# A product with zeros ahead of each group of value products, in the attention of a two-layer encoder

## The chip, the core and the metric

The kernel runs on one core of a Trainium2 chip. The metric is the device time of one execution in microseconds (us), lower being better. The other seven cores are idle.

## What is computed

The reference is a trunk of two layers over 1024 positions of width 1024. Each layer has a mixing part (a gated convolution, six heads of sparse attention, called DSA below, and six heads of banded chunk attention), a cross-attention into 256 memory tokens, and an MLP. The change touches the last product of the two attentions in the mixing part, `p` times `v`:

```python
# chunk attention, one chunk of 64 queries against a band of 9 chunks
s = jnp.einsum('bqhd,bkhd->bhqk', qc, kc).astype(jnp.float32) * scale + bias
s = jnp.where(valid, s, -jnp.inf)
p = jax.nn.softmax(s, axis=-1)
return jnp.einsum('bhqk,bkhd->bqhd', p.astype(vc.dtype), vc)
...
# DSA, one block of 128 queries against the keys that an indexer selected
p = jax.nn.softmax(s, axis=-1)
return jnp.einsum('bhqk,bqkd->bhqd', p.astype(v_sel.dtype), v_sel)
```

## The kernel before

All products run in a form of float32 that the TensorE rounds on reading (F32R), so each factor is split into a high and a low part: `split` lets ScalarE (ACT) write the high part (line 664) and VectorE (DVE) or GpSimd (POOL) subtract it from the source (line 665). An ordinary product of two split factors is three matmuls, `mm3`, lines 340 to 342. Every matmul has its own load of the stationary operand, which the profile shows as the engine PEld.

Per layer the work is: input projections together with the indexer and its top-k selection; then the attention; then the output projection, the cross-attention and the MLP. The attention stage is written as three generators merged by hand: `attention()`, the rest of the mask steps, and `memory`, which projects the memory tokens for the cross-attention and is emitted at a lower priority (`shift(FILL, ...)`) to fill TensorE's gaps.

`attention()` runs `pipeline` over units, first 24 of the chunk attention (six heads, four groups `g` of 256 queries), then 16 of DSA (eight query blocks `b`, two head groups `hg`). A unit has a `scores` part (products, a DVE step that adds the mask and finds the minimum on line 1008, exponentials on ACT on line 1014, division by the row sum on POOL on line 1025) and, three units later, a `values` part.

In `values` the work goes by groups. For one group TensorE transposes blocks of the softmax into a PSUM bank `ps` (line 1145 in the chunk units, 1260 in DSA), `split` makes `ph` and `pl` of it on ACT and DVE, and then the value products (lines 1159 and 1269) add `values x ph` and `values x pl` to the unit's bank `po`. `po` comes from a class of two banks, `ps` from a class of three. In the chunk units the groups number 1, 2, 3 and 3 for `g` = 0 to 3, nine per head, so 54 per layer. In DSA a group is one block of keys `kt`, from 0 to `b`. At the end of a unit ACT copies the lower half of `po` (line 1170 or 1277) and DVE adds the halves (line 1171 or 1284).

Which instruction stands where in an engine's queue is decided at build time: the tile framework plans the whole program with a simulated timeline (`schedule_with_timeline_sim=True`) and priorities that count up with each emitted instruction. An added instruction can therefore also move others. SBUF is handed out by the kernel's own `Arena` of `ARENA` columns; `top=True` takes the highest free place.

Of the kernel before, what the change touches and what calls it, by code (L numbers as in the profile page):

```python
# [13 lines left out]
F32 = mybir.dt.float32  # L14
# [7 lines left out]
P = 128  # L22
# [40 lines left out]
GROUPS = [(7, 6), (5, 4, 3, 2)]  # L63
RES = 10240
BASE = 16512
ARENA = 52736
GRAN = 16


# [241 lines left out]
class Kern:  # L311
    def __init__(self, ctx, tc, a):
# [4 lines left out]
        drp = ctx.enter_context(tc.tile_pool(name="dr", bufs=1, space=bass.MemoryType.DRAM))  # L317
        self.sb = Arena(self.nc, BASE, ARENA)
        self.ps = Banks(psp.tile([P, 8 * 512], F32, name="banks"))
# [25 lines left out]
    def setup(self):  # L345
        nc, sb = self.nc, self.sb
        a = self.a
        self.idf = sb.alloc(P)
        make_identity(nc, self.idf.ap)
        self.flip = sb.alloc(P)  # L350
        nc.gpsimd.memset(self.flip.ap, 0.0)
        nc.gpsimd.affine_select(
            self.flip.ap, self.flip.ap, pattern=[[1, P]], compare_op=ALU.not_equal, fill=1.0,
            base=-(P - 1), channel_multiplier=1,
        )
        self.idr = sb.alloc(P)
        nc.vector.tensor_copy(self.idr.r, self.idf.ap)

# [735 lines left out]
    def chunk_units(self, l, st):  # L1094


        nc, sb = self.nc, self.sb

        def scores(h, g, pts):
            q1, q2, kk, _, bias = st["chk", h]  # L1100
            sm = self.small(2)
            for j, bi in enumerate((2 * g, 2 * g + 1)):
                k0 = max(0, bi - 4) * P
                w = (bi + 1) * P - k0

                def products(ps, s):
                    for i, q in enumerate((q1, q2)):
                        nc.tensor.matmul(
                            ps, q.r[:, bi * P : (bi + 1) * P],
                            kk.r[:, k0 + s.start : k0 + s.stop],  # L1110
                            start=i == 0, stop=i == 1,
                        )

                pts.append(
                    self.softmax(w, products, bias.ap[:, 640 - w : 640], sm[:, j : j + 1])
                )
                if j == 0:
                    self.normalise()
                yield 0.5
            self.rows = (pts, sm)  # L1120

        def values(h, g, pts):
            vv = st["chk", h][3]
            if h % 2 == 0 and g == 0:
                st["y"][5 + h // 2] = sb.alloc(S, top=True)
            y = st["y"][5 + h // 2]
            b = (2 * g, 2 * g + 1)
            k0 = [max(0, x - 4) for x in b]

            both = list(range(k0[1], b[0] + 1))  # L1130
            one = [(kt, 0) for kt in range(k0[0], k0[1])] + [(b[1], 1)]
            groups = [[(both[0], 2)] + one] + [
                [(kt, 2) for kt in both[i : i + 2]] for i in range(1, len(both), 2)
            ]
            po = self.ps.alloc(cls="O")

            for i, group in enumerate(groups):
                ps = self.ps.alloc(cls="T")
                n, todo = 0, []
                for kt, which in group:  # L1140
                    js = (0, 1) if which == 2 else (which,)
                    c = 0 if which == 2 else which * P
                    todo.append((kt, slice(c, c + len(js) * P), slice(n, n + len(js) * P)))
                    for j in js:
                        nc.tensor.transpose(
                            ps.ap[:, n : n + P],
                            pts[j].ap[:, (kt - k0[j]) * P : (kt - k0[j] + 1) * P],
                            self.flip.ap,
                        )
                        n += P  # L1150
                ph, pl = sb.alloc(n), sb.alloc(n)
                self.split(ph.r, pl.r, ps.ap[:, :n])
                self.ps.free(ps)
                todo = [(x, kt, o, s) for kt, o, s in todo for x in (ph, pl)]
                if i == 0:

                    todo.append(todo.pop(1))
                for m, (x, kt, o, s) in enumerate(todo):
                    nc.tensor.matmul(
                        po.ap[:, o], vv.r[:, kt * P : (kt + 1) * P], x.r[:, s],  # L1160
                        start=i == 0 and m == 0,
                        stop=i == len(groups) - 1 and m == len(todo) - 1,
                    )
                sb.free(ph)
                sb.free(pl)
                yield 1.0 / len(groups)
            for x in pts:
                sb.free(x)
            low = sb.alloc(256)
            nc.scalar.copy(low.ap[0:HD, :], po.ap[HD:P, 0:256])  # L1170
            nc.vector.tensor_tensor(
                y.ap[h % 2 * HD : h % 2 * HD + HD, g * 256 : (g + 1) * 256],
                po.ap[0:HD, 0:256], low.ap[0:HD, :], op=ALU.add,
            )
            self.ps.free(po)
            sb.free(low)
            if g == 3:
                for x in st.pop(("chk", h)):
                    sb.free(x)

        for h in range(NH):
            for g in range(4):
                pts = []
                yield (
                    scores(h, g, pts), values(h, g, pts),
                    self.chunk_prepare(l, st, h + 1) if g == 1 and h + 1 < NH else None,
                    0.4 + 0.6 * min(5.0, 2 * g + 1.5),
                )

    def dsa_units(self, l, st):  # L1190


        nc, sb = self.nc, self.sb
# [61 lines left out]
        def values(b, hg, heads):  # L1255
            po = self.ps.alloc(cls="O")
            for kt in range(b + 1):
                ps = self.ps.alloc(cls="T")
                for i in range(3):
                    nc.tensor.transpose(  # L1260
                        ps.ap[:, i * P : (i + 1) * P],
                        heads[i].ap[:, kt * P : (kt + 1) * P], self.idf.ap,
                    )
                ph, pl = sb.alloc(384), sb.alloc(384)
                self.split(ph.r, pl.r, ps.ap[:, :384])
                self.ps.free(ps)
                o = slice(kt * P, (kt + 1) * P)
                for x in (ph, pl):
                    nc.tensor.matmul(
                        po.ap[:, 0:384], st["dv"].r[:, o], x.r,  # L1270
                        start=kt == 0 and x is ph, stop=kt == b and x is pl,
                    )
                sb.free(ph)
                sb.free(pl)
                yield 1.0 / (b + 1)
            low = sb.alloc(384)
            nc.scalar.copy(low.ap[0:HD, :], po.ap[HD:P, 0:384])
            if b == 0 and hg == 0:
                parts = sb.carve(S, S, S)
                y = st["ys"] = sb.tensor(parts[0].off, 3 * S, F32)  # L1280
                for f, x in enumerate(parts):
                    st["y"][2 + f] = Part(x, y[:, f * S : (f + 1) * S])
            y = st["ys"]
            nc.vector.tensor_tensor(
                y.rearrange("p (f s) -> p f s", f=3)[
                    hg * HD : (hg + 1) * HD, :, b * P : (b + 1) * P
                ],
                po.ap[0:HD, 0:384].rearrange("p (f s) -> p f s", f=3),
                low.ap[0:HD, :].rearrange("p (f s) -> p f s", f=3), op=ALU.add,
            )  # L1290
            self.ps.free(po)
            for x in heads + [low]:
                sb.free(x)
# [3 lines left out]
        for b in range(NT):  # L1297
            for hg in range(2):
                heads = []
                yield (  # L1300
                    scores(b, hg, heads), values(b, hg, heads),
                    prepare(b + 1) if hg == 0 and b + 1 < NT else None,
                    0.5 + 1.2 * (b + 1),
                )
# [866 lines left out]
```

## Time and profile before

| | us |
|---|---|
| median of three runs | 3015.66 |
| lowest and highest | 3009.02, 3018.33 |
| the profiled execution, its own time | 3017.18 |
| the profiled execution, its span | 3015.3 |
| mean granted TensorE clock in it, as a share of full speed | 0.982 |
| TensorE matmuls (PE), busy | 2890.9, 96% of the span |
| DVE, ACT, POOL busy | 2160.8, 1559.0, 1310.1 |

The span runs from the first to the last instruction; 1.9 us of the execution's time lie around it. Matmuls are pipelined, so the busy time of a line is more than what its matmuls add to the run: the distance of two starts in a row without gaps is what one costs. The two attention stages lie at 302 to 572 us and at 1792 to 2068 us; in each, the chunk units come first and DSA second.

### The profile page before, as it was taken

The numbers are of one execution on the slowest core, as the hardware profiler recorded it, in microseconds if no ns is written. First come the engines' busy times: TensorE is split into PE (matmuls) and PEld (weight loads), VectorE is DVE, ScalarE is ACT, GpSimd is POOL, SyncE is SP. The second block draws the span as 40 slices with busy tenths as digits, with TensorE's granted clock in tenths as the row PEclk, the third lists the DMA queues.
The fourth block names the chain that finished last, engine by engine and source line by source line (L and its number), as shares of the span: only waits on it lengthen the run. The fifth ranks groups of instructions, "written<-read, shape, count | busy, mean of one in ns | idle before, by whom it ended". The sixth has DMA issues, their size and how long they took to land. (4 is left out here: it accounts for less than half of the span.)

```text
span 3015.3 us, 43469 instructions
## 1 busy us (share of the span) xinstructions
PE 2890.9 (96%) x14440; PEld 2444.5 (81%) x14440; DVE 2160.8 (72%) x4333; ACT 1559.0 (52%) x3146; POOL 1310.1 (43%) x1246
## 2 busy tenths in 40 slices
PE   8999889999999999999999998999999999999998
PEld 7787788788878788888788877887888777888886
DVE  5897886582487766778957987866625877667788
ACT  5676777623234456544457767774232444554442
POOL 4614575522335553232357146754222455533223
PEclk9999999999999999999999999999999999999999
DMA  4213433331334446755412144332213354466544
GB/s 127 63 37 83 103 108 107 101 123 36 113 115 161 170 154 218 247 182 161 162 64 66 36 101 115 96 116 79 107 42 119 102 178 165 152 237 237 181 158 147
DMA packets 265440, 381.99 MB, mean 127 GB/s; under 512 B 23168, under 2 KB 141952, under 8 KB 265216
## 3 DMA queue, kind: packets, MB, share of 16 engines
q1 hardware_dynamic: 265216, 379.22, 38.8%
q8 instruction: 114, 1.87, 0.3%
q14 instruction: 110, 0.90, 0.1%
HBM read 269.56 MB, written 95.42 MB: 121 GB/s over the span
## 5 line engine op out<-in xcount | busy, mean ns | idle before, releaser
L340 PE MATMUL banks<-sb,sb 128*128 128x512 f32 (+3 forms) x3776 | 1425.2, 379 | 23.8 <-ACT sb L664 7.6
L341 PE MATMUL banks<-sb,sb 128*128 128x512 f32 (+3 forms) x3776 | 1420.4, 377 | 11.7 <-POOL sb L286 8.6
L342 PE MATMUL banks<-sb,sb 128*128 128x512 f32 (+3 forms) x3776 | 1416.1, 376 | 7.4 <-POOL sb L665 7.1
L665 POOL TENSOR_TENSOR sb<-sb,sb 128x512 fp32r<-128x512 f32 (+1 forms) x428 | 600.5, 1415 | 913.7 <-ACT sb L664 802.4
L340 PEld LDWEIGHTS banks<-sb,sb 128*128 128x128 f32 x3776 | 715.5, 190 | 156.3 <-ACT sb L664 9.9
L341 PEld LDWEIGHTS banks<-sb,sb 128*128 128x128 f32 x3776 | 715.9, 190 | 135.1 <-POOL sb L286 10.3
L342 PEld LDWEIGHTS banks<-sb,sb 128*128 128x128 f32 x3776 | 713.9, 189 | 133.2 <-POOL sb L665 9.1
L664 ACT CAST sb<-sb 128x512 fp32r<-128x512 f32 (+1 forms) x788 | 455.7, 607 | 594.3 <-PE banks L341 161.5
L286 POOL TENSOR_TENSOR sb<-sb,sb 128x512 fp32r<-128x512 f32 (+2 forms) x288 | 382.6, 1343 | 486.6 <-ACT sb L285 425.3
L665 DVE TENSOR_TENSOR sb<-sb,sb 128x512 fp32r<-128x512 f32 x360 | 274.0, 788 | 38.2 <-ACT sb L664 36.0
L665 DVE TENSOR_TENSOR sb<-banks,sb 128x384 fp32r<-128x384 f32 (+2 forms) x324 | 188.0, 595 | 88.6 <-ACT sb L664 77.0
L285 ACT CAST sb<-sb 128x512 fp32r<-128x512 f32 (+2 forms) x288 | 171.0, 607 | 134.8 <-PE banks L342 30.4
L664 ACT CAST sb<-banks 128x384 fp32r<-128x384 f32 (+2 forms) x324 | 160.1, 518 | 142.9 <-PE banks L1577 75.2
L812 DVE TENSOR_SCALAR_CACHE_REDUCE sb<-sb,sb 128x768 bf16<-128x768 f32 (+3 forms) x256 | 207.5, 810 | 5.0 <-POOL sb L443 2.0
L1741 DVE TENSOR_TENSOR sb<-sb,sb 128x512 f32<-128x512 f32 x160 | 155.2, 1005 | 61.3 <-ACT sb L1721 56.8
L1025 POOL TENSOR_SCALAR sb<-sb,sb 128x128 f32<-128x128 f32 (+7 forms) x192 | 148.5, 789 | 86.4 <-DVE sb L1023 70.0
L1783 DVE TENSOR_TENSOR sb<-banks,sb 128x512 f32<-128x512 f32 x224 | 149.5, 683 | 46.8 <-PE banks L342 45.1
L808 ACT ACTIVATE sb<-sb,sb 128x1024 bf16<-128x1024 f32 (+1 forms) x128 | 140.6, 1099 | 74.3 <-DVE sb L831 64.9
L1846 DVE TENSOR_TENSOR sb<-sb,sb 128x512 f32<-128x512 f32 x128 | 109.5, 858 | 68.7 <-DMA sb<-w_ff_dram 68.2
L1014 ACT ACTIVATE sb<-sb,sb 128x128 f32<-128x128 f32 (+7 forms) x192 | 141.9, 741 | 27.9 <-DVE sb L1008 26.8
L1720 ACT ACTIVATE sb<-sb 128x512 f32<-128x512 f32 x128 | 80.9, 632 | 115.3 <-DVE sb L1783 114.9
L1353 DVE SCALAR_TENSOR_TENSOR sb<-sb,banks 128x512 f32<-128x512 f32 x64 | 43.2, 686 | 114.0 <-PE banks L342 111.4
(173 smaller groups left out, 3055.8 us busy)
## 6 DMA issues: line engine op xcount, KB each, us to landing
sb<-h SPq DMA_DIRECT2D x236, 256.0 KB, 3.2
h<-sb SPq DMA_DIRECT2D x224, 256.0 KB, 2.2
sb<-w_ff_dram SPq DMA_DIRECT2D x216, 256.0 KB, 3.1
sb<-w_ff_dram SPq DMA_DIRECT2D x64, 512.0 KB, 4.0
sb<-w_in_dram SPq DMA_DIRECT2D x64, 256.0 KB, 2.9
sb<-w_mkv_dram SPq DMA_DIRECT2D x64, 256.0 KB, 2.7
sb<-sb SPq DMA_DIRECT2D x54, 256.0 KB, 3.7
xs<-sb SPq DMA_DIRECT2D x24, 512.0 KB, 2.8
```

The costliest lines, as they stand in the source:

```text
L285: k.nc.scalar.copy(hi, st)
L286: k.nc.gpsimd.tensor_tensor(lo, st, hi.bitcast(F32), op=ALU.subtract)
L340: mm(out, lh, rh, start=start, stop=False)
L341: mm(out, lh, rl, start=False, stop=False)
L342: mm(out, ll, rh, start=False, stop=stop)
L664: nc.scalar.copy(hi, src)
L665: eng.tensor_tensor(lo, src, hi.bitcast(F32), op=ALU.subtract)
L812: nc.vector.tensor_scalar(junkb[:, :w], x, c, None, op0=ALU.is_ge, op1=ALU.add, accum_out=n)
L1014: nc.scalar.activation(pt.ap, pt.ap, AF.Exp, bias=mn, scale=-1.0, accum_out=sm)
L1025: nc.gpsimd.tensor_scalar(pt.ap, pt.ap, rc[:, i : i + 1], 0.0, op0=ALU.mult, op1=ALU.add)
L1741: nc.vector.tensor_tensor(z.ap, x, y, op=ALU.add if spec[1] == "+" else ALU.subtract)
L1783: nc.vector.tensor_tensor(r.ap, ps.ap, part[c, x].ap, op=ALU.add)
```

## The change

A tile of zeros, 128 x 256, is made once, at the top of an arena that is larger by just those 256 columns, so the places of all other buffers can stay. In each group of a chunk unit's `values` one matmul with the same stationary block as the group's first product and the zeros as moving operand is emitted between `split` and the products. It writes columns 0 to 255 of `po`; in a unit's first group it carries the start flag, which the first product had before. In DSA the same is emitted for every block of keys but the first, without a start flag. What the other products add is unchanged, since zeros are added.

```diff
-ARENA = 52736
+ARENA = 52992
...
+        self.zero = sb.alloc(256, top=True)
+        nc.gpsimd.memset(self.zero.r.bitcast(F32), 0.0)
         self.idr = sb.alloc(P)
...
                 self.split(ph.r, pl.r, ps.ap[:, :n])
                 self.ps.free(ps)
+
+                nc.tensor.matmul(
+                    po.ap[:, 0:256], vv.r[:, todo[0][0] * P : (todo[0][0] + 1) * P],
+                    self.zero.r, start=i == 0, stop=False,
+                )
                 todo = [(x, kt, o, s) for kt, o, s in todo for x in (ph, pl)]
...
                         po.ap[:, o], vv.r[:, kt * P : (kt + 1) * P], x.r[:, s],
-                        start=i == 0 and m == 0,
-                        stop=i == len(groups) - 1 and m == len(todo) - 1,
+                        start=False, stop=i == len(groups) - 1 and m == len(todo) - 1,
                     )
...
                 o = slice(kt * P, (kt + 1) * P)
+                if kt:
+                    nc.tensor.matmul(
+                        po.ap[:, 0:256], st["dv"].r[:, o], self.zero.r, start=False, stop=False
+                    )
                 for x in (ph, pl):
```

## Rows read from the trace of the kernel before

**Rows 1.** The page: the span, then busy time, share and instructions of each engine.

```profile
span 3015.3 us, 43469 instructions
PE 2890.9 (96%) x14440; PEld 2444.5 (81%) x14440; DVE 2160.8 (72%) x4333; ACT 1559.0 (52%) x3146; POOL 1310.1 (43%) x1246
```

**Rows 2.** Busy time by stage: chunk units, DSA, first and second layer.

```profile
core 0: us, PE busy (x) PEld busy (x) DVE busy (x) ACT busy (x) POOL busy (x), PEclk, DMA share, GB/s
302.00:446.00 144.00, 124.47 (x848) 112.56 (x848) 116.84 (x331) 104.93 (x256) 89.31 (x103) 0.93 0.38 105
446.00:572.00 126.00, 121.45 (x788) 106.54 (x787) 89.58 (x235) 103.78 (x229) 65.70 (x72) 1.00 0.30 97
1792.00:1937.00 145.00, 127.40 (x851) 114.54 (x852) 119.01 (x335) 103.87 (x255) 95.76 (x107) 0.93 0.39 108
1937.00:2068.00 131.00, 122.49 (x777) 107.45 (x776) 93.85 (x239) 103.05 (x225) 69.93 (x73) 0.97 0.30 96
```

**Rows 3.** Groups by line and shape: the value products' counts, busy time and idle before.

```profile
L1269 PE MATMUL banks<-sb,sb 128*128 128x384 f32 x288 | 94.7, 381 | 8.4 <-DVE sb L665 3.9 <-ACT sb L664 3.2
L1159 PE MATMUL banks<-sb,sb 128*128 128x256 f32 x288 | 70.1, 328 | 7.7 <-ACT sb L664 4.3 <-DVE sb L665 3.1
L1159 PE MATMUL banks<-sb,sb 128*128 128x128 f32 x144 | 29.7, 274 | 9.8 <-DVE sb L665 9.5
```

**Rows 4.** Timeline in DSA: first and last of 26 matmuls of 256 columns in a row.

```profile
498.08 0.28 PE L341 MATMUL banks<-sb,sb 128*128 128x256 f32 x1
...
501.08 0.28 PE L342 MATMUL banks<-sb,sb 128*128 128x256 f32 x1
```

**Rows 5.** Busy time, as Rows 2, in stretches within the chunk units.

```profile
302.00:352.00 50.00, 40.63 (x258) 35.72 (x258) 45.34 (x135) 39.23 (x95) 27.15 (x36) 0.90 0.33 89
352.00:372.00 20.00, 19.83 (x165) 19.45 (x164) 12.36 (x33) 10.17 (x20) 9.32 (x12) 1.00 0.61 136
400.00:420.00 20.00, 19.08 (x164) 18.84 (x163) 13.33 (x37) 13.11 (x30) 17.91 (x17) 1.00 0.49 148
1792.00:1848.00 56.00, 45.77 (x282) 39.54 (x283) 51.41 (x149) 40.46 (x99) 30.70 (x37) 0.91 0.34 92
1848.00:1864.00 16.00, 16.00 (x134) 15.89 (x133) 9.28 (x25) 8.46 (x17) 9.77 (x10) 1.00 0.66 146
1888.00:1912.00 24.00, 23.35 (x181) 21.84 (x179) 19.63 (x50) 14.96 (x37) 16.56 (x15) 1.00 0.30 94
```

**Rows 6.** The same stretches, line 1159 alone: PE, PEld, clock, DMA share, GB/s.

```profile
352.00:372.00 20.00, 5.16 (x31) 4.05 (x29) 1.00 0.61 136
400.00:420.00 20.00, 4.20 (x25) 3.34 (x25) 1.00 0.49 148
1848.00:1864.00 16.00, 4.43 (x24) 3.48 (x24) 1.00 0.66 146
1888.00:1912.00 24.00, 4.47 (x28) 3.94 (x28) 1.00 0.30 94
```

**Rows 7.** What ended idle time before line 1269: us, times (matmul and load each).

```profile
  DVE sb L665: 15.3, 37
  ACT sb L664: 10.0, 17
```

**Rows 8.** Busy time, as Rows 2, in 4 us stretches around falls of the clock.

```profile
316.00:320.00 4.00, 2.43 (x17) 2.43 (x18) 4.00 (x11) 3.46 (x9) 3.02 (x4) 0.89 0.13 37
320.00:324.00 4.00, 3.20 (x17) 3.05 (x15) 4.00 (x12) 3.01 (x7) 0.98 (x1) 0.69 0.09 15
...
432.00:436.00 4.00, 0.91 (x4) 0.50 (x4) 4.00 (x8) 1.68 (x7) 1.08 (x3) 0.89 0.00 0
436.00:440.00 4.00, 3.54 (x20) 3.54 (x20) 3.05 (x13) 2.01 (x6) 1.23 (x3) 0.50 0.03 12
```

**Rows 9.** Timeline of DVE and PE around the longest stall before value products.

```profile
433.54 2.29 DVE L886 TENSOR_TENSOR_SCAN sb<-sb 128x1024 f32<-128x1024 f32 x1
435.74 0.67 DVE L665 TENSOR_TENSOR sb<-banks,sb 128x512 fp32r<-128x512 f32 x1
...
436.46 2.29 PE L1159 MATMUL banks<-sb,sb 128*128 128x128 f32 x9 [3.48 <-DVE sb L665]
```

**Rows 10.** POOL's timeline at the start of the run.

```profile
1.94 0.29 POOL L352 TENSOR_SCALAR_AFFINE_SELECT sb<-sb 128x128 f32<-128x128 f32 x1
5.23 3.13 POOL L286 TENSOR_TENSOR sb<-sb,sb 128x296 fp32r<-128x296 f32 x4 [3.01 <-ACT sb L285]
```

**Rows 11.** Waits of PE in 1792 to 2072 us: total, times, longest.

```profile
PE banks L1159 <- DVE sb L665: 6.3, 7, 2.1
PE banks L1108 <- DVE sb L1008: 5.8, 7, 2.4
```

## The prediction, made before the change was run

> **What bounds the kernel now.** I read the page first. TensorE's matmuls are busy for 2890.9 of 3015.3 us [rows 1]: over the run as a whole an added matmul can find little idle time. But the change lies only in the two attention stages, so the next view is busy time by stage. There the reader is to see how the four parts differ: in the chunk units PE is busy for 124.47 of 144 us and 127.40 of 145 us, in DSA for 121.45 of 126 and 122.49 of 131 [rows 2]. Idle PE time is thus 19.5 + 4.6 + 17.6 + 8.5 = 50.2 us, 37.1 of it in the chunk units and 13.1 in DSA. The third view is the chunk units in finer stretches. They fall in two kinds. From 302 to 352 us and from 1792 to 1848 us VectorE is the fuller engine (45.34 of 50 and 51.41 of 56 us) and PE the emptier (40.63 and 45.77). In four other stretches PE leaves 0.17, 0.92, 0 and 0.65 us free of 20, 20, 16 and 24 [rows 5]; that is where the low-priority memory projection fills it. The fourth view is the line of the value products: PE stands idle 7.7 + 9.8 us before line 1159 and 8.4 us before line 1269 [rows 3], waiting for the split on ACT and DVE, as the list of waits says too [rows 11]. The longest of these stalls, 3.48 us, came after a DVE scan of 2.29 us that stood ahead of the split in DVE's queue [rows 9]. Last, the granted clock: 0.93, 1.00, 0.93 and 0.97 in the four parts [rows 2], so it falls from 2.4 to 1.2 GHz now and then, each time after a stretch in which PE had stood idle [rows 8].
>
> **The change part by part.** *How many.* Chunk: 9 groups for each of 6 heads and 2 layers, 108 zero products. The 288 + 144 products of line 1159 [rows 3] are four per group, which agrees. DSA: 288 products of line 1269 [rows 3] are two per block of keys, so 144 blocks; those with kt = 0 (8 query blocks x 2 head groups x 2 layers = 32) get none, which leaves 112. Together 220 matmuls of 256 columns, each with a load.
>
> *What one costs.* The nearest row is a chain of 26 matmuls of 256 columns, each with its own load, without gaps: first start 498.08, last 501.08, so 3.00 us / 25 = 0.120 us [rows 4]. At full price 220 x 0.120 = 26.4 us. From below the bound is nothing, where PE would have waited anyway.
>
> For this price the Trainium skill (TensorE: Matmul & The Clock Gate, Back-to-back issue gap) gives columns / 2.4 plus 2.5 ns for a single matmul, 109 ns at 256 columns. By that the full price would be 24.0 us. The row above was taken with the loads in between, as here, and is the one I use.
>
> *Chunk units.* A zero product needs the values, the zeros and the bank, not the split. It can run as soon as the group's transposes have, in the time in which PE waits for the split; the wait then ends when it did before. In the four full stretches there is no such time: 31 + 25 + 24 + 28 = 108 products [rows 6], 27 groups, x 0.120 = 3.2 us, at full price (they have 1.7 us of room [rows 5]). The other 108 - 27 = 81 groups would cost 9.7 us in full and nothing if hidden; PE has 37.1 - 1.7 = 35.4 us of room there [rows 2, 5], and DVE is the fuller engine. But PE also releases DVE: a zero product ahead of some other transposes or scores delays what DVE and ACT get next. I take a third, 3.2 us, nearer to nothing because DVE has least room in the two largest stretches, and keep 0 and 9.7 for the range.
>
> *DSA.* 112 x 0.120 = 13.4 us in full. PE is 95% busy here (243.9 of 257 us [rows 2]). What can hide a zero product is a stall before its own value products: 37 + 17 = 54 entries are listed for line 1269, for loads and matmuls apart [rows 7], so about 27 stalls for 112 groups, a quarter. The rest, 85 x 0.120 = 10.1 us, is on the path. The ends are 0 (all of it in the 13.1 us of room) and 13.4.
>
> *The clock.* Zero products are work in stretches that have little of it. What the falls cost can be bounded by the parts' mean clock: 0.07 x 144 + 0.07 x 145 + 0.03 x 131 = 24.2 us of full-speed PE time [rows 2]. Some of it is free already, since DVE was busy all the time while the clock was low (4.00 of 4 us from 320 to 324 [rows 8]). Many falls follow one long stall, as at 432 us, where PE was busy for 0.91 of 4 us [rows 8]; a zero product of 0.12 us does not make that stretch full. I count 3 us gained, a few falls fewer; the ends are 0 and 24.2.
>
> *The rest.* The zeros are one POOL step at the start. The nearest row, a POOL step of 128 x 128, takes 0.29 us and is followed by 3.01 us of idle time [rows 10]: nothing, and at most some 0.6 us if the cover were gone. Buffers keep their places. No DMA is added or moved. The first zero product of a unit takes over the wait for the bank `po` that its first product had; behind it on PE stand the next transposes and scores, but there are two such banks, so it should be free. Finally the build-time plan: 220 more matmuls shift its clock, and a long DVE step such as the scan may come to stand before a split or no longer do so. One such stall is worth up to 3.48 us [rows 9]. I expect no sign and give it 6 us either way.
>
> *Sum.* 3.2 + 3.2 + 10.1 - 3 = 13.5 us. The profiled execution took 3017.18 us (span 3015.3), so it becomes 3030.7; it lay 1.5 us above the median of the runs, 3015.66, which becomes 3029.2. I predict **3029 us**.
>
> **The rivals.** *All hidden.* If the splits on ACT and DVE set the pace through the whole stage, the 50.2 us of PE room [rows 2] take in 26.4 us of zero products, and the falls avoided pay for the rest: 3015 to 3018 us. For it speak the stalls before the value products; against it DSA, where ACT and DVE are less busy than PE (103.78 and 89.58 against 121.45 us [rows 2]).
>
> *The clock pays.* This is the case on the other side, faster than before. If the zero products keep the clock up through most stalls, up to 24.2 us of PE time come back. At a gain of 24.2 us, with the price above, the time is 3015.7 + 16.5 - 24.2 = 3008 us; with the chunk price hidden as well, 3015.7 + 10.1 - 24.2 = 3002 us. It decides from the point where the falls avoided give back more than the 16.5 us paid, two thirds of all the clock lost in the stage. For it: in some stretches the clock fell after a moderate gap only (PE busy for 2.43 of 4 us at 316 to 320 [rows 8]), and two groups of zero products there would add 0.24 us. Against it: falls like that at 432 us, with no value product in the idle stretch, and low-clock time that DVE covers.
> The Trainium skill (TensorE: Matmul & The Clock Gate, What's actually happening) says that the throttled state is the default and that activity releases it. By that rule this rival is the one to happen, as far as the zeros count as activity; the falls after idle stretches agree with it, and no row of before shows a product with zeros.
>
> *Full price and more.* If the plan puts the zero products where PE was not waiting, all 220 cost 0.120 us, 26.4 us, and no fall is avoided: 3015.7 + 26.4 = 3042 us; if the moved plan also adds two long stalls of 3.48 us [rows 9], 3049. Against it speaks the room that PE has in the chunk units.
>
> *It does not do what it says.* If the plan were to put the zero products far from the stalls, for instance all of a unit's at its start, the stalls would stay as they are and the price be the one of the rival before.
>
> **How the numbers follow.** Partly hidden, as summed: 0.43. All hidden: 0.23. The clock pays: 0.17. Full price, wherever the zero products stand: 0.17. A measurement of this kernel can tell about 0.3% from no change, 9.0 us, so "same" is 3006.6 to 3024.7. The forecast's own spread is about 8 us (6 for the plan, a few for the shares chosen), which puts somewhat over a quarter of it, 0.12, below 3024.7. Faster: more than half of the clock's 0.17 and a little of the hidden case, 0.13. Same: 0.21 + 0.12 + 0.06 = 0.39. Slower: 0.31 + 0.17 = 0.48. The likeliest case alone spans 3019 to 3039. To leave out no more than 2 in 10, the range goes down to 3005, well into the clock's gain, and up to 3044, over the full price.
>
> **What would show it.** Two new groups in the profile, 108 and 112 matmuls of 256 columns, and 14660 matmuls instead of 14440. Line by line: the idle time before lines 1159 and 1269 should shrink by a few us, the zero products standing before it; DSA (126 and 131 us) should lengthen by about 5 us in each layer, the chunk part (144 and 145) by about 3; the mean clock of the chunk parts should rise from 0.93 by about 0.01 only. Outside the two attention stages nothing should change. I am wrong if DSA does not lengthen (then ACT and DVE set its pace), if the clock in the chunk units goes near 1.00 and the stage shortens, or if a stage without zero products changes by more than a few us, which would be the plan.

## The result, and the profile after

| | us |
|---|---|
| before, median of six runs | 3016.99 |
| after, median of six runs (3028.28 to 3034.88) | 3030.53 |
| after / before | 1.0052, 95% interval 1.0038 to 1.0065 |

The change makes the kernel slower by 13.5 us at the medians, 11 to 20 us by the interval. (The ratio is taken over the runs; that of the two medians is 1.0045.) 3029 was forecast. The sum was right to 2 us; the experiments show that its terms were not.

The page of after, its span and its busy times, answers to [rows 1]:

```profile
span 3027.5 us, 43898 instructions
PE 2905.0 (96%) x14660; PEld 2464.1 (81%) x14660; DVE 2177.8 (72%) x4333; ACT 1561.4 (52%) x3146; POOL 1302.5 (43%) x1247
```

There are 220 more matmuls, as counted, but PE is busy for only 14.1 us more. The groups by line and shape of after answer to [rows 3]. Line 1157 is the zero product of the chunk units and 1275 that of DSA; the value products stand on lines 1166 and 1279 now.

```profile
L1279 PE MATMUL banks<-sb,sb 128*128 128x384 f32 x288 | 98.8, 375 | 7.8 <-ACT sb L666 3.4 <-DVE sb L667 3.3
L1166 PE MATMUL banks<-sb,sb 128*128 128x256 f32 x288 | 71.3, 310 | 5.4 <-DVE sb L667 3.1 <-ACT sb L666 2.0
L1157 PE MATMUL banks<-sb,sb 128*128 128x256 f32 x108 | 33.4, 311 | 1.6 <-DVE sb L1177 1.6
L1275 PE MATMUL banks<-sb,sb 128*128 128x256 f32 x112 | 32.3, 288 | 0.0
L1166 PE MATMUL banks<-sb,sb 128*128 128x128 f32 x144 | 27.9, 260 | 4.2 <-DVE sb L667 3.7
```

The idle time before the chunk units' value products fell from 17.5 to 9.6 us, before DSA's from 8.4 to 7.8. A new wait of 1.6 us stands before line 1157: the first zero product of a unit waiting for its bank, which line 1177 (1171 before) reads. Few zero products stand where the change meant them to: in the trace of after 7 of the 108 in the chunk units, and none of the 112 in DSA, have a wait of TensorE of over 0.05 us straight behind them. The others are followed by the next product at once.

Next the busy time by stage. Here the stages are cut at events and not at round numbers, so that kernels can be compared: from the first score product to the last addition of the chunk units, then to the last addition of DSA, in both layers. Columns as in [rows 2]. First the kernel before, then after.

```profile
297.30:443.50 146.20, 126.34 (x847) 113.74 (x848) 116.94 (x337) 104.99 (x256) 90.70 (x102) 0.91 0.39 108
443.50:579.90 136.40, 131.83 (x836) 115.06 (x835) 98.19 (x248) 106.76 (x236) 68.98 (x75) 1.00 0.30 97
1788.20:1939.20 151.00, 131.65 (x874) 117.50 (x874) 123.78 (x346) 109.52 (x269) 97.69 (x109) 0.93 0.39 107
1939.20:2068.50 129.30, 120.59 (x762) 105.92 (x762) 91.97 (x236) 101.68 (x222) 70.43 (x73) 0.97 0.31 99
sum 562.90, PE 510.41 PEld 452.22 DVE 430.89 ACT 422.94 POOL 327.80; mean PE 127.60 PEld 113.06 DVE 107.72 ACT 105.74 POOL 81.95
```

```profile
297.60:445.70 148.10, 131.61 (x914) 117.76 (x914) 122.97 (x347) 109.17 (x265) 91.46 (x104) 0.96 0.39 107
445.70:586.90 141.20, 135.02 (x883) 122.03 (x884) 96.85 (x238) 104.06 (x226) 66.47 (x74) 1.00 0.30 94
1799.20:1950.10 150.90, 132.56 (x927) 116.97 (x927) 125.84 (x348) 110.58 (x269) 94.45 (x109) 0.99 0.40 107
1950.10:2083.60 133.50, 123.32 (x820) 111.94 (x818) 92.79 (x234) 103.11 (x222) 70.95 (x73) 0.98 0.30 96
sum 573.70, PE 522.52 PEld 468.69 DVE 438.45 ACT 426.92 POOL 323.33; mean PE 130.63 PEld 117.17 DVE 109.61 ACT 106.73 POOL 80.83
```

The two attention stages grew from 562.9 to 573.7 us. DSA grew by 4.8 and 4.2 us, about the 5 expected in each layer; the chunk units by 1.9 and -0.1, less than the 3 expected. Two things don't fit. The granted clock in the chunk units rose from 0.91 and 0.93 to 0.96 and 0.99, far more than the 0.01 I wrote. And the stretch between the two attention stages, where there is no zero product, went from 1208.3 us (579.9 to 1788.2) to 1212.3 (586.9 to 1799.2).

### The profile page after: what moved, and what is told of

Same layout as the page of the kernel before. It is cut to its first block, busy times and chain, and to the rows that moved or that the text cites. A ratio compares the mean times of both kernels' runs of the same rounds, so it can differ in the third digit from the quotient of the medians.

```text
span 3027.5 us, 43898 instructions
## 1 busy us (share of the span) xinstructions
PE 2905.0 (96%) x14660; PEld 2464.1 (81%) x14660; DVE 2177.8 (72%) x4333; ACT 1561.4 (52%) x3146; POOL 1302.5 (43%) x1247
## 5 line engine op out<-in xcount | busy, mean ns | idle before, releaser
L341 PE MATMUL banks<-sb,sb 128*128 128x512 f32 (+3 forms) x3776 | 1421.3, 377 | 13.5 <-POOL sb L286 10.4
L1751 DVE TENSOR_TENSOR sb<-sb,sb 128x512 f32<-128x512 f32 x160 | 155.8, 1009 | 58.1 <-ACT sb L1731 54.0
L1856 DVE TENSOR_TENSOR sb<-sb,sb 128x512 f32<-128x512 f32 x128 | 117.5, 921 | 66.8 <-DMA sb<-w_ff_dram 66.7
L1010 DVE CUSTOM_DVE_ANT_0 sb<-banks,sb 128x128 f32<-128x128 f32 (+5 forms) x192 | 96.3, 508 | 44.7 <-PE banks L1110 17.6
```

The costliest lines, as they stand in the source:

```text
L341: mm(out, lh, rl, start=False, stop=False)
L1751: nc.vector.tensor_tensor(z.ap, x, y, op=ALU.add if spec[1] == "+" else ALU.subtract)
```

## The experiments

The theory on record was the sum: about 0.12 us for each zero product where TensorE is full, nothing where it waits, and a plan that moves with no sign. The rivals were that the moved plan makes the time, and that the clock pays. The kernel before that a run is compared with was timed on the same chip.

**The priorities alone.** The tile of zeros stays, the 220 matmuls go, and the counter that gives the plan its priorities moves on where they stood:

```diff
+                self.tc.cur_priority += 1
...
+                if kt:
+                    self.tc.cur_priority += 1
```

> No zero products, but the tile of zeros and, at each of the 220 places, the priority counter of the plan moved on by one as an added instruction would move it. My theory: the plan barely moves and the time is that of before, 3013 to 3020. If the plan's priorities are what costs: 3025 or more.

Measured: 3017.03 us against 3017.23, ratio 0.9997 (0.9987 to 1.0007). The tile, its POOL step and the shifted priorities cost nothing. They hardly move the order either: compared place by place, 22 of DVE's 4333 instructions differ from before in operation or shape, against 653 in after. If the plan matters, it is through the 220 matmuls that it then has to place.

**One half of the change at a time.** The other half's zero product is left out of the source and the program planned anew; here the edit for the chunk units alone, and the other run leaves out the chunk units' product in the same way.

```diff
-                if kt:
-                    nc.tensor.matmul(
-                        po.ap[:, 0:256], st["dv"].r[:, o], self.zero.r, start=False, stop=False
-                    )
```

> Zero products in the chunk units alone (108 instead of 220), planned anew. My theory (each costs 0.12 us where TensorE is full, nothing where it waits for the split): 2 to 4 us over before, about 3020. If each costs its full price wherever it stands: 13 us over before, 3030. If the zero products pay by keeping the clock up: before or less, 3010 to 3016.

Measured: 3028.44 us against 3017.84, ratio 1.0038 (1.0026 to 1.0050), 10.6 us.

> Zero products in DSA alone (112), planned anew. My theory: TensorE is 95% busy there, so 9 to 11 us over before, 3026 to 3028, and nearly all of what the whole change costs. If the 13.5 us come from a moved plan and not from the products themselves: anything between 3011 and 3023.

Measured: 3029.58 us against 3017.84, ratio 1.0047 (1.0034 to 1.0060), 11.7 us. Each half costs nearly what the whole does: 22.3 us in sum against 13.5. The chunk half costs three times what my theory gave it. A price per product doesn't easily give that; something that each edit sets off once would. In the profile of the chunk half, 5.2 of the 12.1 us that its span grew lie between the two attention stages, where no kernel has a zero product.

**The order of before, with zero products put in afterwards.** To part the plan from the products, the program is planned without zero products, and when the order of every engine is fixed, 220 matmuls are put into TensorE's list. They have no waits of their own and signal nothing.

```diff
+                if first and ahead and not start:
+                    out += [z, j]
+                elif first:
+                    out += [j, z]
...
+    insert(nc, MARKS, ZERO[0].outs[0], True)
     res = run_bass_kernel_spmd(
```

> The planned order of the kernel before, kept to the instruction, and the 220 zero products put into TensorE's queue afterwards, straight ahead of each group's first product (behind it in the first group of a chunk unit), without any wait. My theory: the price is the products' own, so 10 to 17 us over before, 3027 to 3034. If the 13.5 us came from the moved plan: within 3 us of before, 3014 to 3020.

Measured: 3024.48 us against 3017.84, ratio 1.0030 (1.0019 to 1.0041): 6 to 12 us, between the two expectations. In the traces every matmul of before stands in the same order here, and so do all of DVE's and ACT's instructions.

> As the run before it (order of before, 220 zero products put in afterwards), but each one straight behind its group's first product, so that none can run while TensorE waits for that group's split. My theory: what the stalls hid comes on top, some 45 stalls before chunk groups and 27 before DSA blocks x 0.12, so 4 to 8 us over the run with the zero products ahead. If it is only the room in the stage that hides them and not the stall next to them: the same within 2 us.

Measured: 3024.70 us, ratio 1.0026 (1.0016 to 1.0036). Ahead of the group's first product or behind it is the same, as far as the intervals tell, where 4 to 8 us were expected: a zero product is not hidden by the stall next to it. That part of my theory falls, and with it the counting of stalls.

> The planned order of the kernel before with 220 zero products ahead of the groups as in the run with 256 columns, but of 8 columns. If the products' streaming is what made 7 to 9 us there: within 3 us of before, 3014 to 3020. If the clock gives back what the streaming costs, or if the loads and the place in the queue cost: the same 3023 to 3027.

Measured: 3029.12 us against 3016.34, ratio 1.0039 (1.0023 to 1.0055), with runs from 3020 to 3038. That is no less than with 256 columns. So with the order of before the zero products do cost some 0.3%, but this isn't paid for their columns. The clock isn't what costs it: in the timed executions it was 0.982 in the median in both kernels. The traces show that a product of 8 columns takes nearly as much of TensorE as one of 256. From the matmul ahead of a zero product to the second one behind it, at the 143 or 144 places without a gap and at the full clock, it takes 0.105 us more than in before with 8 columns and 0.112 us more with 256.

**The order of after, with other zero products.** Now the program is planned as the changed kernel is, and the zero products are resized in the finished order. All other instructions, and the waits, are those of after.

```diff
-                    self.zero.r, start=i == 0, stop=False,
+                        j, ins=[
+                            cut(x, [list(x.ap[0])] + moving),
+                            cut(v, [list(v.ap[0]), [1, ROWS]]),
+                        ],
+                        outs=[cut(j.outs[0], [[4096, ROWS], [1, n]])], **size,
```

> The planned order of the changed kernel, kept to the instruction, but each zero product cut to 16 moving and 32 stationary columns (a start flag goes back to the first product of a chunk unit). My theory: what they cost goes with their size, so most of the 13.5 us comes back: 3017 to 3022. If the moved plan costs it: 3028 to 3032 stays.

Measured: 3033.73 us against 3017.23, ratio 1.0057 (1.0041 to 1.0072).

> The planned order of the changed kernel; each zero product cut to 8 moving columns, its load of 128 stationary columns left whole. My theory: the distance of 0.12 us between such products is set by the load, so the time stays, 3028 to 3032, or goes up by 1 to 3 us if the clock falls more often with less streamed. If the moving columns set the price: 3017 to 3022.

Measured: 3032.26 us, ratio 1.0054 (1.0039 to 1.0070). The time stayed, as my theory had it. Three timelines show why: first after, then this kernel, then the kernel of the run after next, which has the same order and no zero product; PE in the same place of the order, the columns start, length, engine, line:

```profile
2034.37 0.34 PE L1279 MATMUL banks<-sb,sb 128*128 128x384 f32 x1
2034.54 0.28 PE L1275 MATMUL banks<-sb,sb 128*128 128x256 f32 x1
2034.65 0.34 PE L1279 MATMUL banks<-sb,sb 128*128 128x384 f32 x1
2034.83 0.38 PE L1266 MATMUL banks<-sb,sb 128*128 128x128 f32 x2
```

```profile
2032.60 0.34 PE L1318 MATMUL banks<-sb,sb 128*128 128x384 f32 x1
2032.78 0.17 PE L1314 MATMUL banks<-sb,sb 128*128 128x8 f32 x1
2032.80 0.43 PE L1318 MATMUL banks<-sb,sb 128*128 128x384 f32 x1
2033.07 0.38 PE L1305 MATMUL banks<-sb,sb 128*128 128x128 f32 x2
```

```profile
2035.80 0.51 PE L1334 MATMUL banks<-sb,sb 128*128 128x384 f32 x2
2036.15 0.49 PE L1321 MATMUL banks<-sb,sb 128*128 128x128 f32 x3
```

Behind the zero product of 256 columns the next product starts after 0.11 us, behind the one of 8 columns after 0.02. But the product that follows the narrow one then holds PE for 0.27 us (2032.80 to 2033.07) and not for 0.18. From the value product ahead to the transposes behind it takes 0.46 us with the wide zero product, 0.47 with the narrow one and 0.35 without any: both cost 0.11 to 0.12 us. The distance to the next start, by which I read prices so far, is therefore no price for a narrow product; the distance over its neighbours, less the same without it, is. Read so at the places without a gap and at the full clock, some 160 of the 220, a zero product costs 0.111 us in the mean with 256 columns, 0.088 with 8, and 0.084 in the run before (16 columns, 32 stationary ones). With 8 columns it is least, 0.06, where transposes follow. So these two runs took some 220 x 0.02 = 5 us of TensorE out, and that the time stayed says little about the plan. Below 256 the columns hardly set the price. That the load sets it, as I expected, would fit, but isn't shown: cutting the stationary columns to 32 made the product hardly cheaper.

> The planned order of the changed kernel; each zero product made wider, 512 moving columns in the chunk units and 384 in DSA (0.21 and 0.16 us by columns / 2.4 GHz, against 0.12). My theory: about 0.04 x 112 x 3/4 = 3.4 us more in DSA and 0.09 x 108 x 1/3 = 3.3 us more in the chunk units, 3035 to 3039, with still fewer falls of the clock. If the clock paid for them: no slower than the changed kernel, 3026 to 3031.

Measured: 3041.61 us against 3017.23, ratio 1.0083 (1.0069 to 1.0096), about 9 us over after by the two ratios. Read over its neighbours as above, a wide zero product costs 0.190 us against 0.111, so 220 x 0.079 = 17 us of TensorE were added; half of it shows. The time's answer to size is not a line, but neither is the price: 0.088 us at 8 columns, 0.111 at 256, 0.190 at 384 and 512.

**The order of after, without any zero product.** The 220 matmuls are taken out of the finished order. What one signalled, the matmul before it signals; what one waited for, the matmul behind it waits for.

```diff
+                if j.name in zeros:
+                    gone.add(k)
+                    waits += list(si.on_wait) if si else []
...
+            if gone:
+                b.instructions[:] = [j for k, j in enumerate(b.instructions) if k not in gone]
```

> The planned order of the changed kernel with the 220 zero products taken out of it altogether (what they signalled or waited for is given to their neighbours on TensorE). The runs with shrunken zero products left the time at 1.005 of before. If the moved plan costs that: 3027 to 3034 stays without any zero product. If the mere presence of 220 more instructions costs it: within 4 us of before, 3014 to 3021.

Measured: 3034.40 us against 3016.34, ratio 1.0058 (1.0046 to 1.0070). Without a single zero product, the planned order of the changed kernel is 14 to 21 us slower than that of before, no less than the changed kernel itself. With the products out, the moved plan alone costs as much as the whole change, as far as the intervals can tell. Its stages, cut as above:

```profile
295.80:448.70 152.90, 132.56 (x862) 118.56 (x862) 122.72 (x347) 109.02 (x265) 90.79 (x104) 0.90 0.37 103
448.70:588.10 139.40, 132.66 (x828) 116.97 (x828) 96.95 (x238) 103.91 (x227) 66.51 (x74) 0.98 0.30 95
1800.10:1954.90 154.80, 136.89 (x875) 119.65 (x875) 124.32 (x348) 111.14 (x270) 94.78 (x109) 0.90 0.38 104
1954.90:2083.20 128.30, 117.69 (x762) 104.22 (x762) 91.98 (x234) 102.05 (x221) 70.83 (x73) 0.98 0.31 99
sum 575.40, PE 519.80 PEld 459.40 DVE 435.97 ACT 426.11 POOL 322.91; mean PE 129.95 PEld 114.85 DVE 108.99 ACT 106.53 POOL 80.73
```

575.4 us, against 573.7 with the zero products in. The clock column tells a part of why they are free in this order. The share of clock not granted, times the length, is 0.10 x 152.9 + 0.02 x 139.4 + 0.10 x 154.8 + 0.02 x 128.3 = 36.1 us of full-speed time here; in after it is 0.04 x 148.1 + 0.01 x 150.9 + 0.02 x 133.5 = 10.1. In these two executions the zero products bring back 26.0 us of clock and take 220 x 0.111 = 24.4 us of TensorE. Over all timed executions the balance is less even: the granted clock is 0.983 to 0.986 in after and 0.978 to 0.980 here, some 17 us of full-speed time apart in the mean. What takes in the rest, idle time of TensorE perhaps, is not shown.

**Zero products only where TensorE waits.** If they keep the clock up, they should pay in the places where TensorE stands idle anyway. In the order planned for the kernel with the moved priority counter, which has the time of before, 138 zero products of 256 columns are put in at 17 places. These are the idle gaps of 0.6 us or more that the trace of that kernel shows in the attention stages while a bank of value products is open; each place gets about as many as the gap holds. (The list in the code names more places; those without an open bank get none.)

```diff
+FILL_AT = {1360: 38, 1454: 3, 1458: 10, 1490: 10, 1548: 6, 1552: 5, 1593: 4, ...}
...
+                    n += 1
+                    for _ in range(FILL_AT.get(n, 0) if opened else 0):
+                        v = list(opened.values())[-1]
```

> The planned order of the kernel before, and 138 zero products of 256 columns put in only where TensorE stood idle for 0.6 us or more in an attention stage while a bank of value products was open (17 places, 3 to 26 each, about as many as the gap holds). If falls of the clock cost time in the stage: fewer of them and 2 to 8 us under before, 3009 to 3015. If DVE and ACT cover the low clock: the time of before, 3015 to 3019.

Measured: 3007.67 us against 3016.34, ratio 0.9974 (0.9965 to 0.9983): 5 to 11 us faster than before, and the fastest kernel of this study.

> As the run before it, with 8 columns instead of 256 in each of the 138 products: the same instructions in the same places and hardly any streaming. If the streaming holds the clock up: the falls of before are back and the time is that of before, 3014 to 3019. If the place in the queue matters and not the streaming: the same as with 256 columns.

Measured: 3015.11 us, ratio 0.9999 (0.9987 to 1.0010). The same instructions in the same places with 8 columns gain nothing, so it is the width of the products that gains, not their number or place. The trace shows how, at the longest stall before value products, the one of [rows 9]. First PE's timeline, then 4 us stretches, with 256 columns (line 78 holds both value and zero products there; the columns of the stretches are those of [rows 2]):

```profile
434.40 3.27 PE L78 MATMUL banks<-sb,sb 128*128 128x256 f32 x26
438.05 1.32 PE L78 MATMUL banks<-sb,sb 128*128 128x128 f32 x9 [0.37 <-DVE sb L721]
```

```profile
432.00:436.00 4.00, 3.83 (x29) 3.42 (x30) 4.00 (x10) 3.24 (x12) 2.44 (x6) 1.00 0.25 71
436.00:440.00 4.00, 3.63 (x33) 3.43 (x32) 3.94 (x10) 1.38 (x4) 0.00 (x0) 1.00 0.02 4
```

Then the same with 8 columns:

```profile
432.48 2.96 PE L78 MATMUL banks<-sb,sb 128*128 128x8 f32 x26
436.12 2.06 PE L78 MATMUL banks<-sb,sb 128*128 128x128 f32 x9 [0.69 <-DVE sb L721]
```

```profile
432.00:436.00 4.00, 3.43 (x30) 3.21 (x28) 4.00 (x7) 1.33 (x5) 0.94 (x3) 1.00 0.00 0
436.00:440.00 4.00, 3.88 (x22) 3.88 (x23) 3.09 (x14) 2.57 (x7) 1.40 (x3) 0.57 0.19 69
```

With 26 wide products in the stall the clock stays at 1.00 and the nine value products behind it take 1.32 us. With 26 narrow ones PE is shown as busy too (3.43 of 4 us), and they take nearly as long, 2.96 us against 3.27, yet the clock falls to 0.57 in the next stretch and the same nine take 2.06, near the 2.29 of before [rows 9]. Over the stages the wide fill leaves this:

```profile
298.00:443.00 145.00, 132.16 (x909) 119.28 (x909) 116.82 (x337) 105.05 (x257) 92.06 (x102) 0.93 0.40 109
443.00:579.00 136.00, 131.69 (x839) 115.48 (x839) 97.87 (x248) 106.67 (x236) 68.29 (x75) 1.00 0.31 97
1790.00:1938.60 148.60, 135.79 (x929) 120.71 (x930) 122.60 (x346) 110.11 (x270) 97.52 (x109) 0.95 0.40 109
1938.60:2066.00 127.40, 121.36 (x780) 106.68 (x778) 92.16 (x236) 101.43 (x222) 70.09 (x73) 0.99 0.32 100
sum 557.00, PE 520.99 PEld 462.15 DVE 429.45 ACT 423.27 POOL 327.96; mean PE 130.25 PEld 115.54 DVE 107.36 ACT 105.82 POOL 81.99
```

557.0 us against 562.9. The narrow fill's stages are nearly as short in its one profiled execution (3011.44 us, below its median), so these 6 us alone don't carry the verdict; the timed runs do. In those the granted clock is 0.985 to 0.988 with the wide products and 0.979 to 0.984 with the narrow ones, where before has 0.979 to 0.985. With the wide ones that is some 13 us of full-speed time less lost than in before, and the time is 7 us shorter in the mean. Among the 23 timed executions of before, one us less lost went with about 0.55 us less time, which gives 7 us too.

**Where the moved plan costs.** I measured one more thing on the traces: the stretch between the two attention stages, which has no zero product in any kernel. In the seven kernels with the order of before or one next to it (before, the priorities alone, and the five with products put in afterwards) it lasts 1207.2 to 1210.9 us, 1208.8 in the mean. In the seven whose plan reckoned with zero products it lasts 1210.6 to 1215.0, mean 1212.9. So 4 us of the plan's cost lie outside the attention. Behind the second stage the kernels differ as well (943.6 to 950.2 us), but not by their plan. Most of the rest lies inside: in the order of after without zero products the two chunk parts last 6.7 and 3.8 us longer than before, and more clock is lost (36.1 us against 0.09 x 146.2 + 0.07 x 151.0 + 0.03 x 129.3 = 27.6). Which moved instruction does it stays open; no run put one back.

## Why the prediction was right, and where its steps were not

**The count and the path.** 108 and 112 matmuls, and 14660 in all: right. TensorE as the engine to watch: right.

**The price of one.** 0.120 us from the row of 26 matmuls: right, 0.111 in the mean over the neighbours. But the share of it that I put on the path depends on the order. In the order of before, 220 x 0.112 = 24.6 us of products made 6 to 12 us of time; in the order of after they cost nothing (1.0052 with them, 1.0058 without, the intervals overlapping).

**The chunk units, 3.2 + 3.2 us.** Wrong as a cause. The stage did last only 1.8 us longer in after, but the chunk half alone cost 10.6 us. That the stall next to a product hides it is refuted: ahead of the first product or behind it made 1.0030 and 1.0026.

**DSA, 10.1 us.** The stage grew by 9.0 us and the half alone cost 11.7, as forecast. In the order of after without zero products the two DSA parts last 139.4 and 128.3 us, 2.0 us more than before in sum, so some 7 us of the growth do go with the products there. This term is the one that held best; in the whole it is offset by the chunk units, which are 8.7 us shorter with the products than without.

**The clock, -3 us.** The mis-sized term. I bounded the gain by the 24.2 us that the rows of before show as lost, and then took 3, since a product of 0.12 us doesn't fill a long stall. In the order of after they brought back 26.0 us in the profiled executions and some 17 in the timed ones. How they do it in stretches where few stand next to a wait, these runs don't show. The rival "the clock pays" described the mechanism, and it happened; it paid for a part of the products, and not for the plan.
By the Trainium skill (TensorE: Matmul & The Clock Gate, What's actually happening) activity releases the throttle. The trace agrees: wide zeros in a stall kept 1.00 where narrow ones, just as many, let it fall to 0.57. The wide products streamed nothing but zeros, and the clock stayed up behind them all the same.

**The plan, no sign, 6 us either way.** The term that failed. Without the products the new order costs 18.1 us at the medians (14 to 21), more than the whole change, and the priorities' shift alone is nothing. The split depends on what is taken first: with the order of before the products make 6.6 us at the medians, which leaves 6.9 of the 13.5 to the order. Products and order don't add, but either way the order is not free. I had read no row that could size it, and gave a spread by one stall where the whole order of the stage moves.

**The rest.** POOL's step and the buffers cost nothing: right. The wait for the bank, called free, shows 1.6 us.

So the sum, 13.5, met 13.5 by chance: the products at 16.5 and the clock at -3 were written where the order of after has some 24 us of TensorE and 17 to 26 us of clock, and the plan, 7 to 18 us by the way it is counted, stood at zero.

## What to carry to other kernels

When a planner orders the program, an added instruction is two changes: its own work and another order. Fix the order and vary the work, or keep the work and vary the order, before a cost is put down to either. Read the price of a short instruction over its neighbours, against the same neighbours without it, and not from its own length or the next start. Work that only keeps TensorE's clock up pays if it stands where TensorE waits, in an amount that fills the wait; spread over the groups it was worth no more than it cost.

## What the runs showed of the hardware

In this kernel a matmul of 8 columns with a load of its own was little cheaper than one of 256 columns. At the place shown the next start came 0.02 us behind it and not 0.11, but the one after that came 0.27 us later and not 0.18. Over the neighbours the narrow product cost 0.088 us against 0.111 in the order of after and 0.105 against 0.112 in the order of before, and 26 in a row took 2.96 us against 3.27.

A stretch that the profile shows as busy (3.43 of 4 us, with 26 products of 8 columns in it) was followed by a fall of the clock to 0.57; with 26 products of 256 columns in the same stall the clock stayed at 1.00.
